# Splitting the sixth pair's output store of a sparse 3x3 convolution between SyncE and a GpSimd scatter

## The chip, the core and the metric

The kernel runs on one core of one Trainium2 chip. A time is device time in microseconds (us) of one execution; the figure compared is the median over runs. The profile is of a single execution. TensorE, VectorE, ScalarE and GpSimd compute; SyncE and GpSimd issue DMAs (transfers between HBM and on-chip memory), which 16 DMA engines carry out.

## The reference

A convolution of 16 images of 64 channels, 64x64, with a 3x3 weight that is zero in nine places of ten, to 128 output channels, zero-padded, all float32:

```python
x_pad = np.pad(x, ((0, 0), (0, 0), (pad, pad), (pad, pad)), mode='constant')
...
                        if weight[co, ci, kh, kw] != 0:
                            output[b, co] += weight[co, ci, kh, kw] * x_pad[b, ci, kh:kh+h, kw:kw+w]
```

The kernel makes no use of the zeros: it multiplies with the whole weight.

## The kernel before, in words

**Pairs and blocks.** Two images form a pair: their 2 x 64 channels fill the 128 partitions of `xs`. There are 8 pairs, `p` = 0 to 7; "the sixth pair" is `p` = 5. A pair is worked off in 4 blocks of 16 output rows, so there are 32 blocks, `b` = 0 to 31, and block `b` belongs to pair `b // 4`. The sixth pair is blocks 20 to 23.

**One block.** Even and odd output rows are computed together by a scheme that shares products. GpSimd adds neighbouring input rows into `s` (line 178). ScalarE copies an 18-row window into `win` (line 211). TensorE computes three products (line 292): `ps_p` from `s`, `ps_e` and `ps_o` from `win`. ScalarE copies `ps_p` to `pc` (line 219), and VectorE adds it to `ps_e` and `ps_o` and writes even and odd rows of the output tile `o` (line 248). TensorE's loop runs two blocks per turn; the order of all engines is written by hand, with named semaphores and counts. `s`, `win`, `pc` and `ps_p` have two buffers each. GpSimd's add for block `b` waits (through `p`) until the `ps_p` product of block `b - 2` is done, and TensorE's `ps_p` product of block `b` waits for that add.

**Output tiles.** `o` has three buffers (`N_O` = 3) of 128 output channels x 2 images x 4096 float32, and pair `p` uses buffer `p % 3`. In a tile a partition holds one channel: 16 KB of each of the two images. Pair 5 is the last that uses buffer 2. VectorE waits for the store of pair `p - 3` before it writes pair `p` (semaphores `st0` to `st2`).

**Loads.** The first half of pair 0 is loaded by SyncE as float32 (`x_head`, line 115). All other inputs are loaded and cast to bfloat16 by GpSimd's queue (line 134): pairs 0 to 3 and part of pair 4 at the start, the rest behind the adds of blocks 6, 10, 14, 18 and 22 (the table `AT`). Between the first loads and the first add stand 16 `nop` instructions.

**Stores.** After the last block of a pair (and after block 29) VectorE writes a small `mark` (line 254), which raises the semaphore `r`. SyncE's queue holds the stores in order, each waiting for its mark: pairs 0 to 6 as one DMA of 4 MB each (line 118), pair 7 in two halves of 2 MB (line 124). At the end SyncE waits for the stores in the order `st2`, `st0`, `st1`, `st7`.

Of the kernel before, what the change touches and what calls it, by code (L numbers as in the profile page):

```python
# [17 lines left out]
def kernel(  # L18
# [13 lines left out]
    nc = tc.nc  # L32

    B, C_IN, H, W = x.shape
    C_OUT, _, KH, KW = weight.shape
    assert (B, C_IN, H, W) == (16, 64, 64, 64) and (C_OUT, KH, KW) == (128, 3, 3)
    NP = B // 2
# [4 lines left out]
    N_O = 3  # L42

    pool = ctx.enter_context(tc.tile_pool(name="all", bufs=1))
# [4 lines left out]
    def tiles(n, shape, dtype, name):  # L49
        return [pool.tile(shape, dtype, name=f"{name}{k}") for k in range(n)]  # L50
# [3 lines left out]
    os = tiles(N_O, [C_OUT, 2, H, W], FP32, "o")  # L54
# [6 lines left out]
    w_bf = pool.tile([C_OUT, 3, 4 * C_IN], BF16, name="w_bf")  # L61
    wT = pool.tile([128, 5, 3, C_OUT], BF16, name="wT")
    mark = pool.tile([128, 1], FP32, name="mark")
    ps_p = [psum_pool.tile([128, 2, 8, W], FP32, name=f"ps_p{k}") for k in range(2)]
    ps_e = psum_pool.tile([128, 2, 8, W], FP32, name="ps_e")
    ps_o = psum_pool.tile([128, 2, 8, W], FP32, name="ps_o")
# [3 lines left out]
    def S(name):  # L70
        if name not in sem:
            sem[name] = tc.alloc_semaphore(name)
        return sem[name]

    def after(inst, *waits):
        for name, value in waits:
            inst = inst.wait_op(S(name), value, "sem-ge", check=False)
        return inst

    def pair(p):  # L80
        return x[2 * p : 2 * p + 2].rearrange("n i h w -> (n i) h w")

    def out_of(p):
        return out[2 * p : 2 * p + 2].rearrange("n o h w -> o n h w")
# [15 lines left out]
    def x_sem(p):  # L100
        return f"x{p % 5}"

    X_LANDS = {0: 16, 1: 16, 2: 16, 3: 16, 4: 32, 5: 32, 6: 32, 7: 48}
    HEAD_R, HEAD_C, HEAD_Q = 8, 4, 3
    R_OF = {p: HEAD_R + p + 1 for p in range(NP - 1)}

    with tc.tile_critical(no_gpsimd_drain=True):  # L107
        with nc.Block(no_gpsimd_drain=True) as block:  # L108

            @block.sync  # L110
            def _(sp):
                sp.dma_start(  # L112
                    out=w_sb, in_=weight.rearrange("o i kh kw -> o (i kh kw)")
                ).then_inc(S("w"), 16)
                sp.dma_start(out=x_head, in_=pair(0)[:, 0:HEAD, :]).then_inc(S("xh"), 16)
                for p in range(NP - 1):
                    after(
                        sp.dma_start(out=out_of(p), in_=os[p % N_O]), ("r", R_OF[p])
                    ).then_inc(S(f"st{p % N_O}"), 16)
                p = NP - 1  # L120
                for h in range(2):
                    rows = slice(32 * h, 32 * h + 32)
                    after(
                        sp.dma_start(
                            out=out_of(p)[:, :, rows, :], in_=os[p % N_O][:, :, rows, :]
                        ),
                        ("r", HEAD_R + NP + h),
                    ).then_inc(S("st7" if h else f"st{p % N_O}"), 16)

            @block.gpsimd  # L130
            def _(gp):
                def load(p, a, b, *waits):
                    after(
                        gp.dma_start(out=xs[:, p, a + 1 : b + 1, :], in_=pair(p)[:, a:b, :]), *waits  # L134
                    ).then_inc(S(x_sem(p)), 16)

                load(0, HEAD, H)
                gp.memset(ident, 0.0).then_inc(S("s"), 1)
                after(
                    gp.affine_select(  # L140
                        out=ident,
                        in_=ident,
                        compare_op=mybir.AluOpType.not_equal,
                        fill=1.0,
                        base=0,
                        pattern=[[-1, 128]],
                        channel_multiplier=1,
                    ),
                    ("s", 1),
                ).then_inc(S("s"), 1)  # L150
                for p in range(1, 4):
                    load(p, 0, H)
                load(4, 0, CUT)
                for _ in range(16):
                    gp.nop()

                AT = {
                    6: (4, CUT, H, ("r", R_OF[0])),
                    10: (5, 0, H),
                    14: (6, 0, H),  # L160
                    18: (7, 0, 32),
                    22: (7, 32, H),
                }
                for b in range(NB):
                    p, r0 = b // 4, 16 * (b % 4)
                    waits = []
                    if b == 0:
                        waits.append(("xh", 16))
                    if b == 2 or (b % 4 == 0 and b):
                        waits.append((x_sem(p), X_LANDS[p]))  # L170
                    if b >= 2:
                        waits.append(("p", b - 1))
                    if b < 2:
                        src = x_head[:, r0 : r0 + 16, :]
                    else:
                        src = xs[:, p, r0 + 1 : r0 + 17, :]
                    after(
                        gp.tensor_tensor(  # L178
                            out=ss[b % 2], in0=src[:, 0:16:2, :], in1=src[:, 1:16:2, :], op=ADD
                        ),  # L180
                        *waits,
                    ).then_inc(S("s"), 1)
                    if b in AT:
                        load(*AT[b])

            @block.scalar
            def _(act):
# [126 lines left out]
    done = {f"st{k}": 16 * len([p for p in range(NP) if p % N_O == k]) for k in range(N_O)}  # L314
    for name in sorted(done, key=lambda k: (done[k], k)):
        nc.sync.wait_ge(S(name), nc.sync.to_reg(done[name]), synchronizes=[nc.sync.lower_ap(o[:]) for o in os])
    nc.sync.wait_ge(S("st7"), sixteen, synchronizes=[nc.sync.lower_ap(o[:]) for o in os])


# [28 lines left out]
```

## Time and profile before

| what | value |
|---|---|
| median of 3 runs | 126.47 us (126.14 to 126.97) |
| the profiled execution's own time | 126.21 us |
| its span in the profile | 124.4 us |
| TensorE busy with matmuls | 109.6 us (88%) |
| VectorE, ScalarE, GpSimd busy | 79.2, 69.3, 43.0 us |
| data moved by DMA, mean rate | 42.79 MB, 344 GB/s |
| read from and written to HBM | 17.07 MB, 33.55 MB |
| store of 4 MB, issue to landing (median of 7) | 17.3 us |
| store of 2 MB, issue to landing (median of 2) | 10.3 us |

The page gives each engine's busy time and its share of the span, then the span cut into 40 equal slices with the busy share of each slice in tenths. The line "DMA" is the mean busy share of the 16 DMA engines. "issue to landing" is the time from the DMA instruction to its completion semaphore; it includes the time that the transfer waits behind others. A timeline line has the start and the length in us, then engine, line, operation, tiles and shape, and in brackets the idle time ahead of it with what ended it. The answers on DMA list the packets that start in a window with their bytes; a row of 16 KB is one packet, and each DMA engine closes its share of a DMA with a packet of a few bytes.

### The profile page before, as it was taken

The numbers are of one execution on the slowest core, as the hardware profiler recorded it, in microseconds if no ns is written. First come the engines' busy times: TensorE is split into PE (matmuls) and PEld (weight loads), VectorE is DVE, ScalarE is ACT, GpSimd is POOL, SyncE is SP. The second block draws the span as 40 slices with busy tenths as digits, with TensorE's granted clock in tenths as the row PEclk, the third lists the DMA queues.
The fourth block names the chain that finished last, engine by engine and source line by source line (L and its number), as shares of the span: only waits on it lengthen the run. The fifth ranks groups of instructions, "written<-read, shape, count | busy, mean of one in ns | idle before, by whom it ended". The sixth has DMA issues, their size and how long they took to land.

```text
span 124.4 us, 2437 instructions
## 1 busy us (share of the span) xinstructions
PE 109.6 (88%) x983; PEld 49.1 (39%) x983; DVE 79.2 (64%) x83; ACT 69.3 (56%) x71; POOL 43.0 (35%) x48
## 2 busy tenths in 40 slices
PE   5949999999999999999999999999999999992000
PEld 1414444444444444444444444444444444440000
DVE  2615676777677777777777767775867677775000
ACT  4564666666666666666666666657566666630000
POOL 5564333533353334433343334333333333000000
PEclk9999999999999999999999999999999999999855
DMA  3999999999999999999999999999999999999991
GB/s 85 375 225 213 211 219 219 239 438 338 332 363 432 308 329 324 387 353 345 298 379 408 321 369 427 413 367 348 433 421 432 427 384 427 458 390 416 413 419 71
DMA packets 4179, 42.79 MB, mean 344 GB/s; under 512 B 336, under 2 KB 336, under 8 KB 1104
## 3 DMA queue, kind: packets, MB, share of 16 engines
q1 hardware_dynamic: 2736, 34.90, 67.3%
q0 software_dynamic: 1440, 7.86, 30.6%
q14 instruction: 3, 0.02, 0.0%
HBM read 17.07 MB, written 33.55 MB: 407 GB/s over the span
## 4 chain that ended last, share of the span: by engine, by line
PE 84%; DMA 5%; POOL 1%; DVE 1%; SPq 0%; issue 0%; DVEq 0%
PE ps_e L292 33%; PE ps_o L292 33%; PE ps_p L292 17%; DMA x_head<-in_x_dram 5%; POOL s L178 1%; DVE o L248 1%; SPq L112 0%; SPq L343 0%; SPq L107 0%; DVEq L108 0%
## 5 line engine op out<-in xcount | busy, mean ns | idle before, releaser
L248 DVE TENSOR_TENSOR o<-ps_e,pc 128x1024 f32<-128x1024 f32 x32 | 39.2, 1225 | 31.2 <-ACT pc L219 22.9
L178 POOL TENSOR_TENSOR s<-xs 128x512 bf16<-128x512 bf16 x30 | 34.5, 1150 | 58.0 <-PE ps_p L292 58.0
L211 ACT COPY win<-xs 128x1152 bf16<-128x1152 bf16 (+2 forms) x31 | 34.7, 1121 | 34.2 <-PE ps_o L292 34.2
L292 PE MATMUL ps_e<-win,wT 64*128 64x504 bf16 (+1 forms) x384 | 46.8, 377 | 0.0
L292 PE MATMUL ps_o<-win,wT 64*128 64x504 bf16 (+1 forms) x384 | 46.8, 377 | 0.0
L248 DVE TENSOR_TENSOR o<-ps_o,pc 128x1024 f32<-128x1024 f32 x32 | 38.9, 1216 | 0.1
L219 ACT COPY pc<-ps_p 128x1024 f32<-128x1024 f32 x32 | 32.2, 1006 | 1.8 <-PE ps_p L292 1.8
L292 PEld LDWEIGHTS ps_o<-win,wT 64*128 64x128 bf16 x384 | 18.9, 94 | 22.6 <-DVE o L248 0.2
L292 PEld LDWEIGHTS ps_e<-win,wT 64*128 64x128 bf16 x384 | 18.8, 94 | 22.8 <-DVE o L248 0.8
L292 PE MATMUL ps_p<-s,wT 64*128 64x504 bf16 (+1 forms) x192 | 26.0, 377 | 1.6 <-POOL s L178 1.6
L292 PEld LDWEIGHTS ps_p<-s,wT 64*128 64x128 bf16 x192 | 9.4, 94 | 13.2 <-POOL s L178 2.1
L262 PE MATMUL ps_p<-idle_rhs 128*128 128x512 bf16 x14 | 4.8, 503 | 1.4 <-DVE idle_rhs L225 1.4
L134 POOL DMA_DIRECT2D xs<-in_x_dram x10 | 5.7, 573 | 1.0 <-SPq L107 1.0
L211 ACT CAST win<-x_head 128x1088 bf16<-128x1088 f32 (+1 forms) x3 | 2.3, 811 | 2.8 <-PE ps_o L292 1.6
L178 POOL TENSOR_TENSOR s<-x_head 128x512 bf16<-128x512 f32 x2 | 2.5, 1270 | 2.4 <-DMA x_head<-in_x_dram 2.4
L262 PEld LDWEIGHTS ps_p<-idle_rhs 128*128 128x128 bf16 x14 | 1.5, 117 | 3.4 <-DVE idle_rhs L225 1.4
L91 DVE CAST w_bf<-w_sb 128x192 bf16<-128x192 f32 (+1 forms) x4 | 1.1, 348 | 2.0 <-DMA w_sb<-in_weight_dram 2.0
L91 ACT ACT_TABLE_LOAD x1 | 1.3, 1283 | 0.9 <-SPq L107 0.9
L91 ACT CAST w_bf<-w_sb 128x64 bf16<-128x64 f32 (+1 forms) x2 | 0.7, 415 | 1.7 <-DMA w_sb<-in_weight_dram 1.7
L225 DVE MEMSET idle_rhs<- 128x256 uint32 x1 | 0.3, 272 | 1.1 <-SPq L107 1.1
L232 DVE CAST wT<-ps_e 128x384 bf16<-128x384 f32 x1 | 0.6, 557 | 0.3 <-PE ps_e L267 0.3
L190 ACT CAST wT<-ps_o 128x384 bf16<-128x384 f32 x1 | 0.5, 478 | 0.3 <-PE ps_o L267 0.3
(18 smaller groups left out, 5.4 us busy)
## 6 DMA issues: line engine op xcount, KB each, us to landing
out_dram<-o SPq DMA_DIRECT2D x7, 4096.0 KB, 17.3
xs<-in_x_dram POOLq DMA_DIRECT2D x5, 1024.0 KB, 16.3
out_dram<-o SPq DMA_DIRECT2D x2, 2048.0 KB, 10.3
xs<-in_x_dram POOLq DMA_DIRECT2D x3, 512.0 KB, 13.4
x_head<-in_x_dram SPq DMA_DIRECT2D x1, 1024.0 KB, 5.8
xs<-in_x_dram POOLq DMA_DIRECT2D x1, 640.0 KB, 14.2
xs<-in_x_dram POOLq DMA_DIRECT2D x1, 384.0 KB, 21.2
w_sb<-in_weight_dram SPq DMA_DIRECT2D x1, 288.0 KB, 2.9
```

What stands on the lines that cost most here:

```text
L91: return copy(out=w_bf4[:, g, a:b, :], in_=w_v[:, k : k + b - a, :])
L134: gp.dma_start(out=xs[:, p, a + 1 : b + 1, :], in_=pair(p)[:, a:b, :]), *waits
L178: gp.tensor_tensor(out=ss[b % 2], in0=src[:, 0:16:2, :], in1=src[:, 1:16:2, :], op=ADD),
L190: after(act.copy(out=wT[:, G1], in_=wps(G1)), ("q", 1)).then_inc(S("c"), 1)
L211: act.copy(out=win[b % 2][:, a : a + src.shape[1], :], in_=src), *waits
L219: after(act.copy(out=pcs[b % 2], in_=ps_p[b % 2]), ("p", b + 1)).then_inc(S("c"), 1)
L225: dve.memset(idle_rhs, 0.0).then_inc(S("r"), 1)
L232: after(dve.tensor_copy(out=wT[:, G0], in_=wps(G0)), ("q", 2)).then_inc(S("r"), 1)
L248: dve.tensor_tensor(out=os[p % N_O][:, :, r0 + k : r0 + 16 : 2, :], in0=src, in1=pcs[b % 2], op=ADD),
L262: mm = pe.matmul(idle_ps, idle_rhs[:, 0:128], idle_rhs, start=True, stop=True)
L292: mm = pe.matmul(dst[:, n, :, c_lo:c_hi], tap(g, kw, n), src[q, first : first + 7 * step + 1 : step, c_lo + kw - 1 : c_hi + kw - 1], start ...
```

## The change

Only the store of pair 5 is changed. SyncE stores partitions 0 to 111 of both images in one DMA, and then, in two DMAs of one row of 16 KB each, partition 116 of each image. The other 15 of the last 16 partitions are stored by GpSimd: for each image an indirect DMA (a scatter) with 16 indices in `idx`, of which the one at position 4 is set to 1000 and so is out of bounds and skipped. `idx` is made by an `iota` and an `affine_select` ahead of GpSimd's first add; in return the 16 `nop` become 12. The two scatters stand in GpSimd's queue behind the add of block 25 and wait for pair 5's mark, as SyncE's store does. The end waits for two more semaphores, `sg` for the scatters and `sx` for the single rows, ahead of `st7`.

```diff
@@ -61,6 +61,7 @@
     w_bf = pool.tile([C_OUT, 3, 4 * C_IN], BF16, name="w_bf")
     wT = pool.tile([128, 5, 3, C_OUT], BF16, name="wT")
     mark = pool.tile([128, 1], FP32, name="mark")
+    idx = pool.tile([16, 1], mybir.dt.int32, name="idx")
     ps_p = [psum_pool.tile([128, 2, 8, W], FP32, name=f"ps_p{k}") for k in range(2)]
     ps_e = psum_pool.tile([128, 2, 8, W], FP32, name="ps_e")
     ps_o = psum_pool.tile([128, 2, 8, W], FP32, name="ps_o")
@@ -103,6 +104,14 @@
     X_LANDS = {0: 16, 1: 16, 2: 16, 3: 16, 4: 32, 5: 32, 6: 32, 7: 48}
     HEAD_R, HEAD_C, HEAD_Q = 8, 4, 3
     R_OF = {p: HEAD_R + p + 1 for p in range(NP - 1)}
+    SPLIT, TOP, LEFT = 5, 112, 4
+    out_rows = out.rearrange("n o h w -> (n o) (h w)")
+
+    def o_rows(p, n, a, b):
+        return os[p % N_O].rearrange("o n h w -> o n (h w)")[a:b, n, :]
+
+    def whole(p):
+        return TOP if p == SPLIT else C_OUT
 
     with tc.tile_critical(no_gpsimd_drain=True):
         with nc.Block(no_gpsimd_drain=True) as block:
@@ -114,9 +123,17 @@
                 ).then_inc(S("w"), 16)
                 sp.dma_start(out=x_head, in_=pair(0)[:, 0:HEAD, :]).then_inc(S("xh"), 16)
                 for p in range(NP - 1):
+                    k = whole(p)
                     after(
-                        sp.dma_start(out=out_of(p), in_=os[p % N_O]), ("r", R_OF[p])
+                        sp.dma_start(out=out_of(p)[0:k], in_=os[p % N_O][0:k]), ("r", R_OF[p])
                     ).then_inc(S(f"st{p % N_O}"), 16)
+                    if p == SPLIT:
+                        for n in range(2):
+                            a = TOP + LEFT
+                            row = C_OUT * (2 * p + n) + a
+                            sp.dma_start(
+                                out=out_rows[row : row + 1], in_=o_rows(p, n, a, a + 1)
+                            ).then_inc(S("sx"), 16)
                 p = NP - 1
                 for h in range(2):
                     rows = slice(32 * h, 32 * h + 32)
@@ -151,7 +168,20 @@
                 for p in range(1, 4):
                     load(p, 0, H)
                 load(4, 0, CUT)
-                for _ in range(16):
+                gp.iota(idx, pattern=[[0, 1]], base=0, channel_multiplier=1).then_inc(S("i"), 1)
+                after(
+                    gp.affine_select(
+                        out=idx,
+                        in_=idx,
+                        compare_op=mybir.AluOpType.not_equal,
+                        fill=1000.0,
+                        base=-LEFT,
+                        pattern=[[0, 1]],
+                        channel_multiplier=1,
+                    ),
+                    ("i", 1),
+                ).then_inc(S("i"), 1)
+                for _ in range(12):
                     gp.nop()
 
                 AT = {
@@ -182,6 +212,21 @@
                     ).then_inc(S("s"), 1)
                     if b in AT:
                         load(*AT[b])
+                    if b == 4 * SPLIT + 5:
+                        for n in range(2):
+                            after(
+                                gp.indirect_dma_start(
+                                    out=out_rows,
+                                    out_offset=bass.IndirectOffsetOnAxis(ap=idx[0:16, 0:1], axis=0),
+                                    in_=o_rows(SPLIT, n, TOP, C_OUT),
+                                    in_offset=None,
+                                    element_offset=(C_OUT * (2 * SPLIT + n) + TOP) * H * W,
+                                    bounds_check=15,
+                                    oob_is_err=False,
+                                ),
+                                ("r", R_OF[SPLIT]),
+                                ("i", 2),
+                            ).then_inc(S("sg"), 16)
 
             @block.scalar
             def _(act):
@@ -314,6 +359,8 @@
     done = {f"st{k}": 16 * len([p for p in range(NP) if p % N_O == k]) for k in range(N_O)}
     for name in sorted(done, key=lambda k: (done[k], k)):
         nc.sync.wait_ge(S(name), nc.sync.to_reg(done[name]), synchronizes=[nc.sync.lower_ap(o[:]) for o in os])
+    for name in ("sg", "sx"):
+        nc.sync.wait_ge(S(name), nc.sync.to_reg(32), synchronizes=[nc.sync.lower_ap(o[:]) for o in os])
     nc.sync.wait_ge(S("st7"), sixteen, synchronizes=[nc.sync.lower_ap(o[:]) for o in os])
 
 
```

## The prediction, made before the result was known

> **What bounds the kernel now.** I read the page first, then the busy time by stretch, then the DMA answers for the windows around two store landings, and last the GpSimd, VectorE and SyncE timelines around block 26.
>
> ```profile
> span 124.4 us, 2437 instructions
> PE 109.6 (88%) x983; PEld 49.1 (39%) x983; DVE 79.2 (64%) x83; ACT 69.3 (56%) x71; POOL 43.0 (35%) x48
> ...
> DMA  3999999999999999999999999999999999999991
> ```
>
> TensorE and the 16 DMA engines are both busy nearly all the time, so neither share alone says which sets the end. The stretches do (their columns: time, then busy time of PE, PEld, DVE, ACT, POOL, then clock, DMA share, GB/s):
>
> ```profile
> 50.00:88.00 38.00, 38.00 (x354) 17.16 (x350) 27.90 (x26) 24.10 (x24) 14.43 (x15) 1.00 1.02 368
> 88.00:121.00 33.00, 24.64 (x228) 10.94 (x224) 19.32 (x21) 14.06 (x14) 6.21 (x6) 0.95 0.99 420
> 121.00:124.40 3.40, 0.00 (x0) 0.00 (x0) 0.00 (x0) 0.00 (x0) 0.00 (x0) 0.50 0.26 108
> ```
>
> Until 88 us TensorE never stops. From 88 to 121 us the DMA engines are full (share 0.99, 420 GB/s) while TensorE runs out at 112.65 us (the chain's last matmul). The end is a store, issued at 114.0 us, which lands 9.5 us later although its 2048 KB alone are 16 half rows per engine. The price of one row comes from the window 90 to 100 us: 282 packets, of which 16 are under 512 B, fill 102.0% of 16 engines for 10 us, so one 16 KB row takes 1.02 x 160 / 266 = 0.61 us of one engine, and a half row 0.31 us.
>
> Every store ends with 16 packets under 512 B, one for each engine. The windows 121 to 122 and 122 to 123.2 us show them for the last store:
>
> ```profile
> DMA packets 54, 0.34 MB, mean 336 GB/s; under 512 B 13, under 2 KB 13, under 8 KB 13
> ```
> ```profile
> DMA packets 7, 0.03 MB, mean 27 GB/s; under 512 B 3, under 2 KB 3, under 8 KB 3
> ```
>
> Thirteen engines are done before 122 us and three are not. Four half rows (0.03 MB) start after 122 us; the last busy bin of the second window starts one at 122.69 us, so the last engine ends at 123.0, 1.1 us after the thirteen (about 121.9). Narrower windows have one small packet between 122.45 and 122.9: the second latest engine ends at about 122.5.
>
> The sixth pair's store ends like this (window 101.4 to 102.1 us, 40 bins of 17.5 ns):
>
> ```profile
> GB/s 0 0 0 0 0 0 0 0 936 1873 0 0 0 0 0 0 0 0 0 0 0 0 0 0 0 0 0 0 0 0 0 0 0 936 2809 936 936 936 1872 1872
> DMA packets 27, 0.23 MB, mean 328 GB/s; under 512 B 13, under 2 KB 13, under 8 KB 13
> ```
>
> Again thirteen engines finish by 102.1 us; the next store's rows start only in bin 33, 101.98 us. So the thirteen ran dry for some tenths of a us and waited for the seventh pair's store, and that one waits for VectorE's mark, that is for TensorE. The three late engines (done by 103.2 us) were not dry. After 102 us everything left is pairs 6 and 7: 32 rows x 0.61 = 19.5 us, to about 121.6; with some tenths of slower rows this is the 121.9 seen. So the end is: TensorE's pace to block 27, then 32 rows, then the lateness of the last engine. The last term, 1.1 us, is all that shifting rows among engines can win.
>
> **The change part by part.** The sums are made against the profiled execution (126.21 us, span 124.4, so 1.8 us lie around the span); the median of the runs is 126.47, 0.26 above it, and I add the change to that median.
>
> Rows. Before, the sixth store is 256 rows, 16 per engine. After, SyncE's 112 partitions are 224 rows, 14 per engine if they are dealt evenly; the two scatters bring 15 rows each, and the two single-row DMAs one each. The bytes are the same. If a scatter deals one row to each of 16 engines, the engine whose row is skipped has 14 rows in place of 16: 2 x 0.61 = 1.22 us less. If that is the last engine, it is no longer late at 102 us (there it ended between 102.7 and 102.9, by narrower windows); it cannot start pair 6 earlier than 101.98 us, so about 0.9 us are won on it. Then the second late engine is last, at 122.5: gain 123.0 - 122.5 = 0.5 us. If the hole falls on one of the thirteen, the gain is 0. The single rows add 2 x 16 KB: spread over 16 engines 2 KB each, 0.08 us; left on one engine 1.22 us, of which the dry time of some 0.1 to 0.5 us hides a part. I take 0.08 to 0.1, because the trace's whole stores are all dealt over 16 engines. Sum: -0.5 + 0.1 = -0.4 us.
>
> Shape of the reads. In every store of this trace all 128 partitions are read, and the rows take 0.61 us without visible collisions. A 112-partition store and a 16-partition scatter are not in it. The bound below is 0 (same bytes, same row price). For the bound above, the nearest rows are stretches in which the same queues move less: 338 GB/s from 20 to 50 us, against 420 from 88 to 121; at that rate 4.19 MB take 12.4 instead of 10.0 us, +2.4. The page's poorest full slices move 213 GB/s: 19.7 us, +9.7. Both are stretches of loads and stores mixed, so they are far from this case; I take 0, since the store-only stretch is nearest, and keep the ends. What counts is that only the 0.1 to 0.5 us of dry time absorb it: a later end of this store pushes all that follows one for one.
>
> [...]
>
> GpSimd's queue. The timeline has blocks 24 to 27 here:
>
> ```profile
> 80.88 1.15 POOL L178 TENSOR_TENSOR s<-xs 128x512 bf16<-128x512 bf16 x1 [2.15 <-PE ps_p L292]
> 84.06 1.15 POOL L178 TENSOR_TENSOR s<-xs 128x512 bf16<-128x512 bf16 x1 [2.02 <-PE ps_p L292]
> 87.30 1.15 POOL L178 TENSOR_TENSOR s<-xs 128x512 bf16<-128x512 bf16 x1 [2.09 <-PE ps_p L292]
> 90.68 1.15 POOL L178 TENSOR_TENSOR s<-xs 128x512 bf16<-128x512 bf16 x1 [2.23 <-PE ps_p L292]
> ```
>
> The scatters stand behind block 25's add, free at 85.21 us, and wait for the sixth pair's mark:
>
> ```profile
> 88.20 0.06 DVE L254 MEMSET mark<- 128x1 f32 x1
> ...
> 101.00 0.06 DVE L254 MEMSET mark<- 128x1 f32 x1
> ```
>
> Behind them stands block 26's add, which ran at 87.30 us. TensorE wants its result at 93.02 us (the matmul timeline). It may start at 93.02 - 1.15 = 91.87, so the two scatters may take 91.87 - 88.26 = 3.6 us, 1.8 each. The trace has no scatter; ten load issues on GpSimd cost 0.57 us each, the longest instruction there 1.27 us. Two at 0.57 are 1.1 us, two at 1.27 are 2.5: both fit. I take 0, and keep a stall as a rival. Block 27's add (90.68 us) is needed by 96.3 and comes in time.
>
> Four nops less, an iota and a select more, all before the first add. GpSimd waits 2.44 us there for x_head. The select on 128x128 takes 0.29 us, the memset 0.22; two on 16x1 are under 0.6. Cost 0, under cover of that wait; were it gone, they would delay the first matmul one for one.
>
> SyncE issues two more DMAs at 0.37 to 0.42 us each after 88.67 us; the next thing in its queue is the store that waits for the mark at 101.0. Cost 0. The two waits at the end come ahead of the last one, st7, and are met long before. Cost 0. Who waits for the data: buffer 2 is not written again after the sixth pair, so no add waits for sg or sx. Pair 7's first add, at 98.69 us, waits for the fifth pair's store, which lands by 93.3; the scatter's rows, interleaved with it, can delay it by 2 x 0.61 us. Cost 0.
>
> Sum: -0.4 us on 126.47, 126.1 us.
>
> **The rivals.**
>
> The late read (slower). The odd-shaped store and scatter are read at a lower rate and the store ends after 102 us. For it: never seen here, and the DMA engines show no spare (0.99). Against: row price constant over all stores. It decides once the sixth store needs over 1.8 us more than the 10.0 (0.5 dry, 1.3 for the 1%). Price 2.4 to 9.7 less the dry time; 126.5 + 2 to + 9.5, in the middle 131.
>
> The hole misses. The skipped row belongs to one of the thirteen; the last engine keeps its 16 rows. The trace doesn't name engines, so nothing excludes it; the lateness of 1.1 us being about two rows speaks a little against it. 126.5 + 0.1 = 126.6 us.
>
> GpSimd holds TensorE. A scatter takes over 1.8 us; at 3 us each block 26 is 2.4 us late, the mark at 101.0 too, and with it the last stores; the last engine absorbs up to 0.9. 126.5 + 1.5 to + 2.4, some 128.3.
>
> The single rows stay on one engine: 14 + 2 + 2 rows, 1.22 us late in place of the engine relieved; 126.6 us.
>
> **How the numbers follow.** The last engine relieved 0.35; the late read 0.34; the hole misses 0.18; GpSimd holds TensorE 0.06; single rows on one engine 0.04; something outside these, faster, 0.03, since the 1.1 us of lateness is less than 1%. About 1% is what a measurement of this kernel can tell from no change. Within 1%: 0.35 + 0.18 + 0.04 = 0.57; slower 0.40; faster 0.03. The predicted time is the likeliest case's, 126.1, with its own range 125.4 (all 1.1 us won) to 127.0. The range of 8 in 10 takes in the lower half of the late read: 125.4 to 131.5 leaves out about 0.17 above and 0.03 below.
>
> **What would show it.** The last store's small packets: fifteen or sixteen before 122.3 us if the late engine is relieved, still one near 123.0 if the hole missed. The seventh pair's first rows at about 102 us, with thirteen or more engines dry before, if the split store is read at full rate; no gap there, GB/s well under 420 between 89 and 102, and later landings for all that follows, if not. A wait of TensorE on GpSimd's s at 93 us would show the third rival. My prediction is wrong if the sixth store ends after 102.5 us on most engines.

## The result, and the profile after

The changed kernel took 132.77 us (median of 4 runs), the kernel before 126.72 us beside it: a ratio of 1.044, 95% interval 1.034 to 1.054. Times here are medians of all runs, but the ratios and intervals leave out runs more than 1.5% above the fastest of their kernel, and the profile of the partition halves below is of such a run. In a later comparison the ratio was 1.030 (1.023 to 1.036), and the ten runs of the changed kernel on record spread from 129.7 to 138.9 us, so the loss itself varies from run to run. The forecast was 126.1 us, no change; the time lies above the stated range, 125.4 to 131.5 us.

The profiled execution of the changed kernel took 132.49 us, its span is 130.7. The page, to compare with the lines of before:

```profile
span 130.7 us, 2452 instructions
PE 109.6 (84%) x983; PEld 48.7 (37%) x983; DVE 79.2 (61%) x83; ACT 69.2 (53%) x71; POOL 45.2 (35%) x52
...
DMA  3999999999999999999999999999999999999940
...
out_dram<-o SPq DMA_DIRECT2D x1, 3584.0 KB, 21.1
```

TensorE has the same 109.6 us of work, GpSimd 2.2 us more. The DMA engines move the same 42.79 MB, but they are full until about 124 us in place of 121 and then run down slowly. So the bytes take longer. The stretches show where (columns: time, then busy time of PE, PEld, DVE, ACT, POOL, clock, DMA share, GB/s). The kernel before:

```profile
94.00:102.00 8.00, 8.00 (x78) 3.61 (x74) 5.37 (x7) 5.42 (x6) 3.44 (x3) 1.00 0.94 403
102.00:110.00 8.00, 8.00 (x78) 3.62 (x74) 6.22 (x7) 4.13 (x4) 1.15 (x1) 1.00 1.00 422
...
118.00:124.00 6.00, 0.00 (x0) 0.00 (x0) 0.00 (x0) 0.00 (x0) 0.00 (x0) 0.50 0.65 272
```

The changed kernel:

```profile
94.00:102.00 8.00, 8.00 (x78) 3.61 (x74) 6.09 (x7) 5.56 (x6) 3.04 (x3) 1.00 1.01 331
102.00:110.00 8.00, 8.00 (x78) 3.61 (x74) 5.50 (x6) 4.76 (x5) 1.56 (x2) 1.00 1.01 354
...
118.00:124.00 6.00, 0.00 (x0) 0.00 (x0) 0.00 (x0) 0.00 (x0) 0.00 (x0) 0.50 1.01 423
```

From 94 to 110 us the engines are as busy as ever (1.01) and move 331 and 354 GB/s in place of 403 and 422. TensorE keeps its 8.00 us in both stretches, so no matmul waits. The window 94 to 108 us of the changed kernel gives the price of a row (q1 holds the DMAs that SyncE issues, q0 those of GpSimd):

```profile
DMA packets 336, 4.68 MB, mean 334 GB/s; under 512 B 50, under 2 KB 50, under 8 KB 50
## 3 DMA queue, kind: packets, MB, share of 16 engines
q1 hardware_dynamic: 271, 4.18, 82.8%
q0 software_dynamic: 64, 0.49, 18.1%
```

Of 336 packets 50 are small and one is an instruction fetch: 285 rows in 1.009 x 16 x 14 = 226 us of engine time, 0.79 us a row. Before, it was 0.61. That is 285 x 0.18 / 16 = 3.2 us for the average engine. The scatter's rows are the worst: 0.49 MB, 30 rows, in 0.181 x 224 = 40.5 us, 1.35 us each.

The rest of the loss is unevenness. The window 124.4 us to the end:

```profile
DMA packets 86, 0.58 MB, mean 92 GB/s; under 512 B 15, under 2 KB 15, under 8 KB 15
```

The page of before counts 336 packets under 512 B for 21 DMAs, 16 each; they are taken as the closing packets, one for each of the 16 engines. Before, thirteen engines ended within 0.2 us (121.8 to 122.0) and the last 1.1 us after them. Now fifteen closing packets start after 124.4 us, one after the other, the last after 129.3 us; from 128.5 us on only one is still to come, and its engine works alone, on two half rows. About 0.9 us of the profile's 6.3 are not the change's: in this execution the first input landed later (`x_head` took 6.6 us from issue to landing, in place of 5.8 before and of 5.6 and 5.5 in the two runs with the scatters alone, whose GpSimd code up to the first add is that of the change), so that GpSimd's first add started at 8.13 us in place of 7.26, and TensorE's work is shifted by as much.

GpSimd went as forecast (its timeline, blocks 25 to 27):

```profile
84.92 1.16 POOL L208 TENSOR_TENSOR s<-xs 128x512 bf16<-128x512 bf16 x1 [2.02 <-PE ps_p L337]
89.42 0.91 POOL L218 DMA_INDIRECT out_dram<-o,idx  x1 [3.35 <-DVE mark L299]
90.64 0.88 POOL L218 DMA_INDIRECT out_dram<-o,idx  x1 [0.30 <-issue]
91.53 2.28 POOL L208 TENSOR_TENSOR s<-xs 128x512 bf16<-128x512 bf16 x2
```

Block 26's add ends at 92.7 us, and TensorE's product for it starts at 93.88, on its usual pace: the wait for the mark and the two scatters are hidden.

### The profile page after: what moved, and what is told of

Same layout as the page of the kernel before. It is cut to its first block, busy times and chain, and to the rows that moved or that the text cites. A ratio compares the mean times of both kernels' runs of the same rounds, so it can differ in the third digit from the quotient of the medians.

```text
span 130.7 us, 2452 instructions
## 1 busy us (share of the span) xinstructions
PE 109.6 (84%) x983; PEld 48.7 (37%) x983; DVE 79.2 (61%) x83; ACT 69.2 (53%) x71; POOL 45.2 (35%) x52
## 2 busy tenths in 40 slices
DMA packets 4215, 42.79 MB, mean 327 GB/s; under 512 B 372, under 2 KB 372, under 8 KB 1140
## 4 chain that ended last, share of the span: by engine, by line
PE 80%; DMA 5%; POOL 1%; DVE 1%; SPq 0%; issue 0%; DVEq 0%
PE ps_e L337 32%; PE ps_o L337 32%; PE ps_p L337 16%; DMA x_head<-in_x_dram 5%; POOL s L208 1%; DVE o L293 1%; SPq L121 0%; SPq L390 0%; SPq L116 0%; DVEq L117 0%
## 5 line engine op out<-in xcount | busy, mean ns | idle before, releaser
L218 POOL DMA_INDIRECT out_dram<-o,idx x2 | 1.8, 895 | 3.7 <-DVE mark L299 3.4
```

The lines of the kernel that those rows point to most:

```text
L218: gp.indirect_dma_start(out=out_rows, out_offset=bass.IndirectOffsetOnAxis(ap=idx[0:16, 0:1], axis=0), in_=o_rows(SPLIT, n, TOP, C_OUT), i ...
```

## The experiments

Three theories stood at the start. **A**: the rows of an odd set of partitions are read by several DMA engines at once and slow each other. **B**: GpSimd's queue or the scatter is slow. **C**: the rows are dealt unevenly, the single rows above all. The code cuts show only the lines that differ for the sixth pair, with the constants written in and the waits left out.

**The 16 partitions by SyncE in place of the scatter.**

```diff
+ sp.dma_start(out=out_of(p)[0:112], in_=os[p % N_O][0:112])
+ sp.dma_start(out=out_of(p)[112:128], in_=os[p % N_O][112:128])
```

> The sixth pair's store as two SyncE DMAs, partitions 0 to 111 and 112 to 127; no scatter, no single rows, GpSimd as before the change. Theory A (the odd shapes: rows of few or unevenly spread partitions are read by several DMA engines at once and slow each other): still slow, 130 to 134 us, and rows longer than 0.61 us after 92 us. Theory B (the GpSimd queue: a scatter's rows are slow or hold up SyncE's rows, the narrow store is innocent): back to 126 to 127 us. Theory C (uneven dealing: the two single rows on one engine, the skipped row): 126 to 127 us, as each engine has 16 rows again.

Measured: 132.38 us, ratio 1.052 (1.046 to 1.057). No GpSimd part, no hole, no single rows, and as slow as the change. B and C cannot explain this. The window 100 to 106 us has 106 packets, 26 of them small, in 107.2% of 96 us of engine time:

```profile
DMA packets 106, 1.31 MB, mean 218 GB/s; under 512 B 26, under 2 KB 26, under 8 KB 26
## 3 DMA queue, kind: packets, MB, share of 16 engines
q1 hardware_dynamic: 106, 1.31, 107.2%
```

So an average row takes 1.072 x 96 / 80 = 1.29 us while the 16 partitions are stored. At most 32 of these 80 rows are theirs, so the window does not give the price of theirs alone.

**The 112 partitions alone.**

```diff
+ k = 112 if p == 5 else C_OUT
+ sp.dma_start(out=out_of(p)[0:k], in_=os[p % N_O][0:k])
```

> Only partitions 0 to 111 of the sixth pair are stored, by SyncE; partitions 112 to 127 of that pair are left out, so 2 of 16 rows per engine (1.2 us) fewer. Theory A: the narrow store alone loses more than the missing rows give, 127 to 130 us. Theories B and C: 126 to 126.5 us, a little under before, since the engines only stay dry longer before the seventh pair's store.

Measured: 126.24 us, ratio 1.000 (0.997 to 1.003). That is what B and C expected, and less than A did. In its window 94 to 100 us a row takes 1.015 x 96 / 146 = 0.67 us:

```profile
DMA packets 146, 2.39 MB, mean 399 GB/s; under 512 B 0, under 2 KB 0, under 8 KB 0
## 3 DMA queue, kind: packets, MB, share of 16 engines
q1 hardware_dynamic: 146, 2.39, 101.5%
```

The narrow store pays 0.06 us a row, 14 x 0.06 = 0.8 us per engine, and stores 1.2 us less: by this sum it ends 0.4 us before the whole store did, and the engines were dry for a while there anyway (70 GB/s from 101.4 to 102.1 us in this run). So the narrow rows are slower, as A has it, but by themselves they are not what costs 6 us; the 16 partitions are, or the meeting of both.

**The scatters alone**, beside a SyncE store of all partitions.

```diff
- sp.dma_start(out=out_of(p)[0:k], in_=os[p % N_O][0:k])
+ sp.dma_start(out=out_of(p)[:, :, 0:56], in_=os[p % N_O][:, :, 0:56])
  gp.indirect_dma_start(
-     out=out_rows,
+     out=side,
```

> SyncE stores all 128 partitions of the sixth pair but only 56 of 64 image rows (the last 8 are left out), the same bytes as the 112 partitions. The two scatters read the same 16 partitions as in the change and write to a side buffer in HBM. No single rows. Theory A: the scatter has a price of its own because its 16 partitions are read by all engines at once, 127.5 to 130 us, rows of the software queue again over 1 us. Theory B: the whole loss is here, 131 to 133 us. Theory C: 126 to 127 us.

Measured: 129.02 us, ratio 1.019 (1.012 to 1.026). Window 92 to 98 us:

```profile
DMA packets 144, 1.73 MB, mean 289 GB/s; under 512 B 27, under 2 KB 27, under 8 KB 27
## 3 DMA queue, kind: packets, MB, share of 16 engines
q0 software_dynamic: 50, 0.49, 59.7%
```

Thirty rows take 0.597 x 96 = 57 us, 1.9 us each. The scatter alone costs 1.9%, about 2.4 us.

**The same rows by SyncE, together and spread.** Two kernels that differ in one slice. Both store 56 of 64 image rows of all partitions and then 16 partitions whole, to a side buffer:

```diff
+ sp.dma_start(out=out_of(p)[:, :, 0:56], in_=os[p % N_O][:, :, 0:56])
+ sp.dma_start(out=side, in_=os[p % N_O][112:128])      # together
+ sp.dma_start(out=side, in_=os[p % N_O][0:128:8])      # spread
```

> SyncE stores all 128 partitions of the sixth pair but 56 of 64 image rows (the last 8 are left out), then by a second DMA the 32 rows of partitions 112 to 127, to a side buffer in HBM; GpSimd as before the change. Bytes as before the change. If the price comes from 16 neighbouring partitions being read by all 16 engines (theory A), SyncE pays it as GpSimd does: 129 to 133 us, rows far over 0.61 us around 100 to 106 us. If it is GpSimd's queue (theory B), 126 to 127 us.

> As the run with the rows of partitions 112 to 127, but the second DMA reads every eighth partition (0, 8, ... 120): the same number of rows, bytes, DMAs and engines, and the same place in HBM. If neighbouring partitions are what collides (theory A), a good part of the loss goes: 126.5 to 129 us, and the longest rows are shorter. If any small DMA behind a store, or the writing side in HBM, is the cause, the same time as that run within 0.7 us.

Measured: together 128.66 us, ratio 1.019 (1.010 to 1.027); spread 126.94 us, 1.003 (1.000 to 1.007). Their DMA issues (size, then us from issue to landing), together:

```profile
out_dram<-o SPq DMA_DIRECT2D x1, 3584.0 KB, 13.9
side<-o SPq DMA_DIRECT2D x1, 512.0 KB, 17.0
```

Spread:

```profile
out_dram<-o SPq DMA_DIRECT2D x1, 3584.0 KB, 13.8
side<-o SPq DMA_DIRECT2D x1, 512.0 KB, 14.7
```

The two intervals do not overlap. The same DMAs, the same number of rows and bytes, the same destination, the same engine issuing. Only which partitions are read differs. The main store lands alike (13.9 and 13.8 us); the 512 KB take 3.1 us longer than it from neighbouring partitions and 0.9 us longer from spread ones. The queue, the small size of the DMA and HBM's side are the same in both, so they cannot make this difference; which partitions are read together is shown to matter.

**The scatter from spread partitions.**

```diff
-     return os[p % N_O].rearrange("o n h w -> o n (h w)")[a:b, n, :]
+     return os[p % N_O].rearrange("o n h w -> o n (h w)")[0:128:8, n, :]
```

> The run with the scatters alone, but the scatters read every eighth partition in place of 112 to 127 (writes to the same side buffer; SyncE's store leaves out the last 8 image rows). Theory A: faster than with neighbouring partitions (129.0 us), 126.5 to 128 us, software queue rows well under 1.6 us. Theory B: 128.5 to 129.5 us, unchanged.

Measured: 127.19 us, ratio 1.007 (1.003 to 1.012). The loss of the scatter alone falls from 1.9% to 0.7% through this one slice. Its window 92 to 98 us:

```profile
DMA packets 187, 2.25 MB, mean 375 GB/s; under 512 B 34, under 2 KB 34, under 8 KB 34
## 3 DMA queue, kind: packets, MB, share of 16 engines
q1 hardware_dynamic: 126, 1.75, 75.0%
q0 software_dynamic: 60, 0.49, 25.2%
```

The thirty rows take 0.252 x 96 / 30 = 0.81 us each, not 1.9. B is out as the main cause. What the 0.7% that is left comes from, no run shows.

**The store in halves, by partition and by image.** Two kernels with the same number of DMAs, rows and bytes:

```diff
+ sp.dma_start(out=out_of(p)[0:64], in_=os[p % N_O][0:64])                # by partition
+ sp.dma_start(out=out_of(p)[64:128], in_=os[p % N_O][64:128])
...
+ sp.dma_start(out=out_of(p)[:, 0:1], in_=os[p % N_O][:, 0:1])            # by image
+ sp.dma_start(out=out_of(p)[:, 1:2], in_=os[p % N_O][:, 1:2])
```

> The sixth pair's store by SyncE in two DMAs, partitions 0 to 63 and 64 to 127; all bytes, no GpSimd part. Theory A: each half uses only a part of what 128 partitions give, so the two take clearly longer than 10 us: 130 to 136 us, rows of about 1.2 us. If only an uneven dealing or the narrow 16 partitions matter: 126 to 127 us. [...]

> The sixth pair's store by SyncE in two DMAs, one for each image, all 128 partitions in both; all bytes. It has the same number of DMAs, rows and bytes as the run with partitions 0 to 63 and 64 to 127. Theory A (partitions): as before the change, 126 to 126.8 us. If splitting a store in two is what costs: 130 us or more.

Measured: by partition 135.85 us, ratio 1.071 (1.061 to 1.081); by image 126.33 us, 0.999 (0.996 to 1.002). Partition halves, window 96 to 100 us:

```profile
DMA packets 52, 0.85 MB, mean 213 GB/s; under 512 B 0, under 2 KB 0, under 8 KB 0
## 3 DMA queue, kind: packets, MB, share of 16 engines
q1 hardware_dynamic: 52, 0.85, 103.0%
```

Image halves, window 94 to 100 us:

```profile
DMA packets 172, 2.56 MB, mean 426 GB/s; under 512 B 16, under 2 KB 16, under 8 KB 16
```

Sixty-four partitions gave half the rate, 213 against 426 GB/s, with all 16 engines "busy" (103%): a row takes 1.03 x 64 / 52 = 1.27 us, twice 0.61. At half the rate 4.19 MB take 9.8 us more; the ratio of 1.071 is 9 us. Splitting a store cost nothing by itself (by image, ratio 0.999).

**The single rows.** The changed kernel without them, twice, the second time beside the changed kernel:

```diff
- sp.dma_start(out=out_rows[row : row + 1], in_=o_rows(p, n, a, a + 1))
```

> The changed kernel without SyncE's two single-row DMAs (those two rows are left out). The profile of the change shows one completion update for each of them, so each lies on one engine and is worth 0.61 us there, if it is the same engine for both 1.2 us. Theories A and B: 131 to 132.8 us, at most 1.2 us under the change. Theory C: 127 to 128 us.

> The changed kernel once more, beside the run without its single rows. All theories: 131.5 to 133.5 us.

> The changed kernel without the two single-row DMAs (those rows are left out), on the same chip as the changed kernel, since the first run of it spread too widely (129.4 to 137.1 us). If the single rows cost only their own 2 x 0.61 us on one engine: 0 to 1.2 us under the changed kernel. If their row, read from the same neighbouring partitions, holds up others too: 1.5 to 3 us under it.

Measured: the first time 132.14 us, but from 129.4 to 137.1 us and without an interval, inconclusive. In the second comparison 131.28 us, ratio 1.031 (1.023 to 1.038), the changed kernel 131.69 us, 1.030 (1.023 to 1.036). The single rows cost nothing that these runs resolve, which is to about 1.3 us by the two intervals. C is out as the main cause.

**The seventh pair's store in halves, in the kernel before.** This tests the prediction's chain: were the engines dry before 102 us, and is the end set by the late ones?

```diff
- if b % 4 == 3 or b == NB - 3:
+ if b % 4 == 3 or b in (NB - 7, NB - 3):
```

> The kernel before, but the seventh pair's store in two halves, as the eighth's, with one more mark after block 25. All bytes. If the prediction's chain holds (the engines run dry for 0.1 to 0.5 us before the seventh store, and the last engine is not dry but late): the gap at 102 us is gone and 0 to 0.5 us are won, 125.8 to 126.5 us. If the engines were not dry: no change, 126.3 us.

Measured: 126.44 us, ratio 1.000 (0.997 to 1.003). Window 101 to 103 us:

```profile
DMA  9907799090709873339793739993099993099993
...
DMA packets 96, 0.82 MB, mean 410 GB/s; under 512 B 16, under 2 KB 16, under 8 KB 16
```

The gap at 102 us is gone: rows start throughout. Nothing is won. This is what follows if the engines that were dry are not the ones that end last: in this run too, 13 closing packets of the last store come between 121 and 122 us and three after 122. The time alone decides nothing, since both expectations contain it; that the gap was there and is gone is read from the traces.

## Why the prediction was wrong

**The step that failed** is "Shape of the reads": "Both are stretches of loads and stores mixed, so they are far from this case; I take 0, since the store-only stretch is nearest, and keep the ends." The store-only stretch was nearest in kind of transfer, but it reads all 128 partitions in each store, and that is the very thing that the change alters. The runs put in its place: 0.06 us more a row for the 112-partition store, 1.35 us a row for the scatter's rows of 16 neighbouring partitions (1.9 in the run with the scatters alone), 0.79 us for the average row from 94 to 108 us, all against 0.61 before. On top of the slower rows came the unevenness of the engines, 5 us at the end in place of 1.1, which the prediction had only as something to win. The rival "the late read" had place and direction right, and its price holds the measured loss (2.4 to 9.7 us less the dry time; measured 6.1 by the medians, 5.6 by the ratio). That it does is partly luck: its two ends come from stretches of loads and stores mixed, the upper one from a slice read as 213 GB/s where the page's poorest full slice has 211. The range was cut at the rival's lower half, 131.5 us, and the time was 132.77.

What the runs show in the place of the taken 0 is a rate that goes with the partitions read together: the halves by partition moved 213 GB/s, half of the 426 of the halves by image, and 512 KB from 16 neighbouring partitions took 3.1 us longer to land than the main store, from 16 spread ones 0.9 us longer. Why the partitions read together decide, no run shows.

**Which engine is late, and the hole.** Whether the skipped row's hole falls on the late engine was not seen: the engines' ends are spread over 5 us, and a gain of 0.5 us, which no run shows, could not be seen in that.

**The chain at the end.** Right: the dry engines at 102 us were there, and removing the gap won nothing, as it should if the late engines set the end. Right too that only some tenths of us would absorb a later sixth store: the changed kernel's rows run on without a gap at 102 us, and the time grew by far more.

**GpSimd's queue.** Right: the scatters took 0.91 and 0.88 us, between the 0.57 and 1.27 taken as bounds and under the 1.8 that would have held TensorE. The iota and the select took 0.12 and 0.25 us, ahead of the first input. The rival of a held TensorE fell.

**SyncE's queue.** The end was right, a size wrong: the single-row DMAs took 1.2 and 1.5 us of the queue, not 0.4, and were out of it at 92.3 us, well before the seventh store at 101.95. The trace has a single completion update for each of them (372 packets under 512 B, and 370 in the runs with the scatters alone, which have the same DMAs but for these two), where a DMA dealt over all engines has 16, so each is read as lying on one engine; the prediction took the other case. It did not decide.

**The parts and the whole.** The 112-partition store costs 0.8 us per engine, the 16 partitions by themselves 2.3 us of time, and both in one store 6.1 us. The traces show where the rest lies. After 122 us the kernel before has 0.03 MB left to move; by the slices of their profile pages the run with the rows together has about 1.0 MB and the run with 112 and 16 partitions about 1.5 MB. At 420 GB/s this is 2.3 and 3.5 us more for the average engine, and 3.5 is near 0.8 + 2.3. What is left is unevenness: with the rows together the engines are full until 123.0 us and at 3 tenths in the last slice of the page (161 GB/s, to 126.2 us); with 112 and 16 partitions they are at 5 tenths from 123.6 to 126.9 us (224 GB/s) and under one tenth from there to 130.1 us (35 GB/s). Why they end so unevenly stays open. That the 112-partition store throws the engines out of step, so that they meet the slow rows at different times, would explain it, but was not tried.

## What to carry to other kernels

In these runs a store's time depends on the set of partitions that its rows come from, not on bytes and engines alone: keep all 128 partitions in each transfer, and cut along the free dimension where a transfer must be cut (halves by image 126.33 us, halves by partition 135.85, the uncut store beside them 126.42 and 126.37). A DMA share of 1.0 did not tell the rate (it was 1.01 here at 331 GB/s and 1.00 at 422); compare GB/s and the time of a row before believing that nothing is lost. When a change alters a property that every transfer of the trace has in common, the trace's constant price is no evidence for the new case, and the range must hold the whole rival.

## What the runs showed of the hardware that was not expected

The loss outlasted its store: in the changed kernel the rate was back at 423 GB/s from 118 to 124 us, but the engines ended unevenly all the same, with fifteen closing packets between 124.4 and 129.4 us. Nor did an engine take over another's share: after 128.5 us two half rows still started on the last engine, when the other fifteen had closed theirs.
